# Seven block products in the first output projection, and partial results that accumulate in one bank

## The chip, the cores and the metric

The kernel runs on one core of a Trainium2 chip. The metric is device time in microseconds (us) of one execution. Engines in the profile are PE (TensorE matmul), PEld (TensorE weight load), DVE (VectorE), ACT (ScalarE), POOL (GpSimd) and SP (SyncE, which here only issues DMAs); `SPq` and `POOLq` are their DMA queues.

## The reference

Two layers on 528 tokens (16 learned ones ahead of 512) of width 2048. Each layer is `h + post_norm(mixer(pre_norm(h)))`, with RMS norms. Layer 0 is grouped-query attention with a gate, layer 1 a chunked gated linear attention. The part that the change touches is the last line of the attention, and the norm around it:

```
    return (o * jax.nn.silu(gate)) @ w_out                  # attention_mixer, w_out 2048 x 2048
    ...
        h = h + rmsnorm(y, post_norm[i])
```

`rmsnorm(y, w)` divides by the root of the mean square over the width, and multiplies by `w`.

## The kernel before

**Operands.** Activations lie transposed: width on the 128 partitions in 16 blocks (k), 528 tokens in the free dimension, in two halves of 264. Each is kept as two float32r parts: `uh`, the rounded value, and `ul`, the rest. A weight block is loaded in float32 (`wraw`, 512 KB, two buffers), and split by ScalarE into `whi` and by VectorE into `wlo` (three buffers each; `weights`, `split`). Every product is three matmuls: hi·hi, lo·hi and hi·lo.

**Plain columns.** `project` computes 128 output columns: for each token half 16 blocks of k by three matmuls into one of the three PSUM banks of `ps_p` (tag `pp`), and an evacuation.

**Seven products.** `seven` computes a pair of 128-column tiles for all tokens with a Strassen-Winograd scheme: the weight is cut into four 128x1024 blocks a11, a21, a12, a22 (columns by halves of k), the activation into four by halves of k and of the tokens. Sums and differences of the weight blocks are made by VectorE (`sums`), those of the activation once by `combine` (T1 to T4, split into `th`, `tl`). Seven block products, each 8 blocks of k by three matmuls of 128x264, replace eight. The results are added on VectorE (`add`) to SBUF tiles y1, y2. It is used for five pairs of the gate in layer 0 (about 106 to 208 us) and six pairs of values in layer 1 (about 1030 to 1152 us).

**Around the change.** The output projection of layer 0 runs from about 750 to 945 us. Its first two columns are a `group`: while it runs, the gated heads are reloaded from DRAM (`og_d`) and split into `uh`, `ul`, block by block. Columns 2 to 12 are plain. For columns 13 to 15 all first token halves come first and then all second halves, so that the norm of the first half can begin; the first three of their six weight units go to tiles of their own (`own`). For each column, `squares` copies the bank into `hs[m]` with the post-norm scale, squares it, and GpSimd adds the square to `acc`. Then `mean_rsqrt` and `residual` (which loads the old h through quarters of the tiles x0, x1) make the new h and its split, while layer 1's first columns are projected.

**Order.** The program is recorded by one pass; `clk` is a clock of estimated TensorE time that places the side work. A priority scheduler then fixes the order on each engine: weight loads and splits are recorded with a lead (`AHEAD`), so that they stand ahead of the work around them. An engine runs its instructions in that order and waits at each for its semaphores.

Of the kernel before, what the change touches and what calls it, by code (L numbers as in the profile page):

```python
# [19 lines left out]
P = 128  # L20
# [62 lines left out]
def hybrid_encoder(  # L83
# [22 lines left out]
    kq_d = scratch.tile([4, P, T], F32, name="kq_d")  # L106
    v_d = scratch.tile([5, P, D], F32, name="v_d")


# [9 lines left out]
    def col(i):  # L119
        return cols[:, i:i + 1]  # L120
# [71 lines left out]

    def combine(th, tl, xs):

        for k in range(KH):
            x = xs[k % len(xs)]
            u = [t[:, k:k + KH + 1:KH].bitcast(F32) for t in (uh, ul)]
            V.tensor_tensor(x.rearrange("p (j t) -> p j t", j=2), *u, op=ALU.add)
            q = x.rearrange("p (j t) -> p j t", j=4)
            V.tensor_tensor(q[:, 0:2], q[:, 1::2], q[:, 0:2], op=ALU.subtract)  # L200
            V.tensor_tensor(q[:, 3], q[:, 3], q[:, 0], op=ALU.subtract)
            V.tensor_tensor(q[:, 2], q[:, 2], q[:, 3], op=ALU.subtract)
            split(th[:, k], tl[:, k], x)
            yield 2.4

    def seven(src, c, ys, th, tl, free):

# [13 lines left out]
        def sums(o, a, b, op=ALU.subtract):  # L221
            with tc.high_priority(AHEAD):
                V.tensor_tensor(o, a, b, op=op)

        def product(w, b):
            ps = ps_p.tile([P, 512], F32, tag="pp", name="pp")[:, :HALF]
            bh, bl = b
            for k in range(KH):
                PE.matmul(ps, w[0][:, k], bh[:, k], start=k == 0, stop=False)  # L229
                PE.matmul(ps, w[0][:, k], bl[:, k], start=False, stop=False)  # L230
                PE.matmul(ps, w[1][:, k], bh[:, k], start=False, stop=k == KH - 1)  # L231
                clk.step(3 * (HALF + 7) / 2400)
            return ps
# [19 lines left out]
        A.copy(y1[:, l], product(w, of_u(0, 0)))  # L253
# [246 lines left out]
    fr = pool(la, "fr0")  # L500
    ps_s = pool(ps0, "ps_s", space=PSUM)
    ps_t = pool(ps0, "ps_t0", 2, space=PSUM)
    ps_o = pool(ps0, "ps_o", space=PSUM)

# [38 lines left out]
    for h in range(3, 13, 2):  # L543
        ys = y_tiles()
        free = seven(w_in0, 4096 + h * P, ys, th, tl, free)
        for i in range(2):
            nc.gpsimd.dma_start(out=g_d[h + i], in_=ys[i])
    clk.finish(first)
    clk.flush()
    la.close()  # L550


# [226 lines left out]
    yp = pool(la, "yp", 2)  # L779
    quarters = [yp.tile([P, 4 * HALF], F32, name=f"x{i}", bufs=1) for i in range(2)]  # L780


# [3 lines left out]
    hs = [tp.tile([P, T], F32, name=f"h{k}") for k in range(KT)]  # L786
    acc = tp.tile([P, T], F32, name="acc")
    r0 = tp.tile([P, T], F32, name="r0")
# [14 lines left out]
    def squares(m, ps, a, b):  # L803
        A.activation(hs[m][:, a:b], ps, AF.Copy, scale=col(POST + m))
        if m == 0:
            A.activation(acc[:, a:b], ps, AF.Square)
            return
# [6 lines left out]
    for m, ps, a, b in banks0:  # L814
        squares(m, ps, a, b)
    ps0.close()
    ps_g = pool(tr, "ps_g1", space=PSUM)
# [158 lines left out]
    sa = pool(la, "sa", 2)  # L976
    ps_v = pool(la, "ps_v", 2, space=PSUM)
    th, tl = [ta.tile([P, KH, 4 * HALF], F32R, name=f"t{w}") for w in "hl"]
    quarters += [ta.tile([P, 4 * HALF], F32, name=f"x{i}") for i in range(2, 4)]
# [34 lines left out]
    for vc in range(2, 14, 2):  # L1014
        ys = y_tiles()
        free = seven(w_in1, 2048 + vc * P, ys, th, tl, free)
        clk.drive(token_rows(ys, vc))
# [429 lines left out]
```

## Time and profile before

| | before |
|---|---|
| runs | 1787.76, 1788.43, 1789.2 us; median 1788.43 |
| span of the profiled execution | 1784.8 us, core clock 0.996 |
| TensorE / VectorE / ScalarE / GpSimd busy | 98% / 63% / 53% / 16% |
| bytes moved by DMA | 200.95 MB, 113 GB/s on average |

The profile was taken of one execution, whose span goes from the first to the last instruction; the runs' times contain some microseconds around it. In the groups of instructions, a line such as `L130 DVE TENSOR_TENSOR wlo<-wraw,whi 128x1024 ... x239 | 292.7, 1226 | 300.5 <-ACT whi L129 299.0` has the source line, the engine, the operation with output and inputs, the count, busy time in us, mean ns of one, and the idle time ahead of them with what ended it. In the DMA list the last number of a row is the median time in us from issue to landing.

### The profile page before, as it was taken

Reading aid. Unit: us, or ns where it says so; the run is one execution under the profiler, and the core shown is the slowest. Engines: PE = TensorE matmul, PEld = TensorE weight load, DVE = VectorE, ACT = ScalarE, POOL = GpSimd, SP = SyncE. Lnnn points to the kernel's source line nnn. Section 1 sums busy time; section 2 is a strip of 40 time slices with the busy share of each in tenths; the row PEclk is TensorE's granted clock in tenths of the full one; section 3 lists DMA queues with packets and bytes.
Section 4 is the critical chain, followed back from the end, with each engine's and each line's share of the span. In section 5 each row is a group of like instructions: output and inputs, shape, how many; then the busy total and the mean of one; then the engine's idle time right before and its main releaser. Section 6 shows DMA issues by size and latency. Waiting matters only on the chain.

```text
span 1784.8 us, 31606 instructions
## 1 busy us (share of the span) xinstructions
PE 1753.4 (98%) x12591; PEld 1653.0 (93%) x12591; DVE 1126.2 (63%) x1883; ACT 951.4 (53%) x1912; POOL 292.8 (16%) x392
## 2 busy tenths in 40 slices
PE   8999999999999999999999999999999999999998
PEld 8999999999999999999999899988888989888886
DVE  5888776667676666722247987667684865764224
ACT  5644455556556455632347444478685765853222
POOL 3113015323423322111111001110000000000000
PEclk9999999999999999999999999999999999999999
DMA  8444423223233233343336344343332332344333
GB/s 257 139 126 134 124 78 102 85 83 107 74 96 93 76 97 104 121 117 95 96 93 195 118 141 121 99 138 88 87 108 84 103 94 86 103 144 177 95 95 130
DMA packets 265124, 200.95 MB, mean 113 GB/s; under 512 B 9772, under 2 KB 239856, under 8 KB 264448
## 3 DMA queue, kind: packets, MB, share of 16 engines
q1 hardware_dynamic: 251600, 159.00, 31.1%
q0 software_dynamic: 13376, 39.93, 6.6%
q8 instruction: 99, 1.62, 0.4%
q14 instruction: 49, 0.40, 0.1%
HBM read 164.39 MB, written 28.01 MB: 108 GB/s over the span
## 4 chain that ended last, share of the span: by engine, by line
PE 75%; ACT 2%; DVE 2%; issue 1%; DMA 0%; POOL 0%; DVEq 0%; ACTq 0%; SPq 0%
PE pp L152 15%; PE pp L154 15%; PE pp L153 15%; PE f L1359 2%; PE f L1357 2%; PE f L1358 2%; PE pp L229 2%; PE pp L231 2%; PE pp L230 2%; PE pT L654 1%; PE o L1177 1%; PE o L1178 1%; PE o L1176 1%; PE s L636 1%; PE s L637 1%; PE s L638 1%
## 5 line engine op out<-in xcount | busy, mean ns | idle before, releaser
L152 PE MATMUL pp<-uh,whi 128*128 128x264 f32 (+1 forms) x2320 | 713.4, 308 | 1.0 <-POOL whi L363 0.9
L153 PE MATMUL pp<-ul,whi 128*128 128x264 f32 (+1 forms) x2320 | 703.1, 303 | 1.5 <-DVE ul L425 1.5
L154 PE MATMUL pp<-uh,wlo 128*128 128x264 f32 (+1 forms) x2320 | 703.6, 303 | 0.3 <-POOL wlo L364 0.3
L130 DVE TENSOR_TENSOR wlo<-wraw,whi 128x1024 fp32r<-128x1024 f32 (+1 forms) x239 | 292.7, 1226 | 300.5 <-ACT whi L129 299.0
L154 PEld LDWEIGHTS pp<-uh,wlo 128*128 128x128 f32 x2320 | 438.1, 189 | 17.5 <-POOL wlo L364 0.6
L152 PEld LDWEIGHTS pp<-uh,whi 128*128 128x128 f32 x2320 | 438.1, 189 | 17.4 <-POOL whi L363 1.2
L153 PEld LDWEIGHTS pp<-ul,whi 128*128 128x128 f32 x2320 | 438.6, 189 | 15.4 <-DVE ul L425 2.0
L129 ACT CAST whi<-wraw 128x1024 fp32r<-128x1024 f32 (+1 forms) x239 | 248.8, 1042 | 294.2 <-PE pp L153 108.7
L293 POOL DMA_DIRECT2D qs<-qw x96 | 48.3, 508 | 255.9 <-ACT sq L287 219.7
L129 ACT CAST whi<-x 128x1024 fp32r<-128x1024 f32 x48 | 50.2, 1049 | 58.7 <-PE pp L230 35.9
L644 ACT ACTIVATE pn<-s,mx 128x528 f32<-128x528 f32 (+1 forms) x72 | 50.2, 697 | 50.9 <-DVE mx L641 50.9
L231 PE MATMUL pp<-uh,wlo 128*128 128x264 f32 x264 | 75.2, 285 | 0.5 <-DVE wlo L130 0.5
L1359 PE MATMUL f<-whi,ul 128*128 128x512 f32 x192 | 75.6, 394 | 0.0
L1357 PE MATMUL f<-whi,uh 128*128 128x512 f32 x192 | 75.5, 393 | 0.0
L1358 PE MATMUL f<-wlo,uh 128*128 128x512 f32 x192 | 75.3, 392 | 0.0
L229 PE MATMUL pp<-uh,whi 128*128 128x264 f32 x264 | 75.0, 284 | 0.0
L230 PE MATMUL pp<-ul,whi 128*128 128x264 f32 x264 | 74.8, 283 | 0.0
L130 DVE TENSOR_TENSOR wlo<-x,whi 128x1024 fp32r<-128x1024 f32 x48 | 60.5, 1263 | 15.7 <-ACT whi L129 15.6
L641 DVE TENSOR_REDUCE mx<-s 128x1 f32<-128x528 f32 (+1 forms) x72 | 50.6, 703 | 28.7 <-PE s L638 28.1
L659 DVE TENSOR_TENSOR pl<-pT,ph 128x512 fp32r<-128x512 f32 (+1 forms) x80 | 47.3, 592 | 17.5 <-ACT ph L658 16.7
L229 PE MATMUL pp<-th,whi 128*128 128x264 f32 x192 | 56.1, 292 | 0.8 <-ACT th L129 0.8
L658 ACT CAST ph<-pT 128x512 fp32r<-128x512 f32 (+1 forms) x80 | 40.8, 510 | 29.0 <-PE pT L654 24.6
(413 smaller groups left out, 3762.7 us busy)
## 6 DMA issues: line engine op xcount, KB each, us to landing
wraw<-in_attn_w_in_dram SPq DMA_DIRECT2D x82, 512.0 KB, 4.1
wraw<-in_gla_w_in_dram SPq DMA_DIRECT2D x81, 512.0 KB, 3.9
wraw<-in_attn_w_out_dram SPq DMA_DIRECT2D x32, 512.0 KB, 3.8
wraw<-in_gla_w_out_dram SPq DMA_DIRECT2D x32, 512.0 KB, 3.8
x<-in_gla_w_in_dram SPq DMA_DIRECT2D x15, 512.0 KB, 4.1
qs<-qw POOLq DMA_DIRECT2D x96, 66.0 KB, 3.9
x<-in_attn_w_in_dram SPq DMA_DIRECT2D x12, 512.0 KB, 4.6
x<-h_d SPq DMA_DIRECT2D x32, 132.0 KB, 3.5
```

Of the source, the lines that this page charges most:

```text
L129: A.copy(hi, src)
L130: V.tensor_tensor(lo, src, hi.bitcast(F32), op=ALU.subtract)
L152: PE.matmul(ps, wh, uh[:, k, a:b], start=first, stop=False)
L153: PE.matmul(ps, wh, ul[:, k, a:b], start=False, stop=False)
L154: PE.matmul(ps, wl, uh[:, k, a:b], start=False, stop=last)
L229: PE.matmul(ps, w[0][:, k], bh[:, k], start=k == 0, stop=False)
L230: PE.matmul(ps, w[0][:, k], bl[:, k], start=False, stop=False)
L231: PE.matmul(ps, w[1][:, k], bh[:, k], start=False, stop=k == KH - 1)
L641: V.reduce_max(mx, s, axis=AX.XY, negate=True)
L1357: PE.matmul(ps, uh[:, k, ts], wh[:, kk], start=(k == 0), stop=False)
L1358: PE.matmul(ps, uh[:, k, ts], wl[:, kk], start=False, stop=False)
L1359: PE.matmul(ps, ul[:, k, ts], wh[:, kk], start=False, stop=(k == KT - 1))
```

## The change

Three things are done.

1. Layer 0's output columns 5 to 12 become four pairs by `seven`. `combine` gets its operands in part from DRAM: for the first six of the eight k, GpSimd's queue loads the two raw blocks from `og_d` into x0, x1 and two more tiles, while columns 0 to 4 are still computed plainly.
2. The raw outputs of columns 0 to 12 are copied to tiles y0, y1, squared from there, and stored to a scratch tensor `y_d`. After the pairs they are loaded into `hs`, whose memory is used by the pairs' operands until then. The post-norm scale moves to `residual`. The first loads of the old h, the loads for the low-rank gates (`wr`) and the memset of `wl` come behind the pairs.
3. In `seven`, for all 15 pairs, products that share partial sums accumulate in a bank: P1, T2, T3 and T4 in one bank of `pp` (p1), with a copy or an addition out of it after each, and T1 and the last difference in a bank of new pools (`ps_x`, tag `x`, p5).

```diff
-    def combine(th, tl, xs):
-
+    def combine(th, tl, xs, raw=None, n_raw=0, pace=2.4):
+
+        def load(k):
+            if k < n_raw:
+                nc.gpsimd.dma_start(out=xs[k % len(xs)].rearrange("p (j t) -> p j t", j=2),
+                                    in_=raw[k:k + KH + 1:KH].rearrange("j p t -> p j t"))
+        for k in range(len(xs)):
+            load(k)
         for k in range(KH):
...
-            V.tensor_tensor(x.rearrange("p (j t) -> p j t", j=2), *u, op=ALU.add)
+            if k >= n_raw:
+                V.tensor_tensor(x.rearrange("p (j t) -> p j t", j=2), *u, op=ALU.add)
...
-            yield 2.4
-
-    def seven(src, c, ys, th, tl, free):
+            load(k + len(xs))
+            yield pace
+
+    def seven(src, c, ys, th, tl, free, ps_x):
...
-        w = parts(a11)
+        w1 = parts(a11)
         sums(s, a21, a22, ALU.add)
+        w5 = parts(s)
         sums(a21, a11, a21)
         sums(a11, s, a11)
-        A.copy(y1[:, l], product(w, of_u(0, 0)))
-        add(y1[:, r], product(parts(a11), of_t(T2)), y1[:, l])
-        add(y2[:, r], product(parts(a21), of_t(T3)), y1[:, r])
-        add(y2[:, l], product(parts(a22), of_t(T4)), y2[:, r])
-        p5 = product(parts(s), of_t(T1))
-        add(y2[:, r], p5, y2[:, r])
+        w2 = parts(a11)
+        p1 = ps_p.tile([P, 512], F32, tag="pp", name="pp")[:, :HALF]
+        product(w1, of_u(0, 0), p1)
+        A.copy(y1[:, l], p1)
+        p5 = product(w5, of_t(T1))
+        A.copy(y2[:, r], p5)
+        product(w2, of_t(T2), p1, True)
+        A.copy(y1[:, r], p1)
+        add(y1[:, l], product(parts(a12), of_u(1, 0)), y1[:, l])
+        sums(a11, a12, a11)
+        product(parts(a21), of_t(T3), p1, True)
+        add(y2[:, r], p1, y2[:, r])
+        product(parts(a11), of_u(1, 1), p5, True)
         add(y1[:, r], p5, y1[:, r])
-        w = parts(a12)
-        sums(a11, a12, a11)
-        add(y1[:, l], product(w, of_u(1, 0)), y1[:, l])
-        add(y1[:, r], product(parts(a11), of_u(1, 1)), y1[:, r])
-        return [spare, a21, a22, s, a12, a11]
+        product(parts(a22), of_t(T4), p1, True)
+        A.copy(y2[:, l], p1)
+        return [spare, s, a21, a11, a12, a22]
...
+    ys = [y_tile(i) for i in range(2)]
+    for m, ps, a, b in banks0:
+        A.copy(ys[m][:, a:b], ps)
+        outgoing(m, ys[m], a, b)
+    ps0.close()
+    ps_x = pool(sx, "ps_x2", 4, space=PSUM)
+    built = clk.drive(combine(th, tl, xs, og_d, 6, 3.0))
+    for m in range(2, 5):
+        y = y_tile(m % 2)
+
+        def plain(ps, a, b):
+            A.copy(y[:, a:b], ps)
+            outgoing(m, y, a, b)
+        project(w_out0, m * P, HALVES, plain)
+    clk.finish(built)
+    free = [wpool.tile([P, 1024], F32, tag="wraw", name="wraw", bufs=2) for _ in range(2)]
+    free += [q[:, :1024] for q in xs]
+    for m in range(5, KT - 3, 2):
+        ys = [y_tile(i) for i in range(2)]
+        free = seven(w_out0, m * P, ys, th, tl, free, ps_x)
+        for i in range(2):
+            outgoing(m + i, ys[i], 0, T)
+    sx.close()
...
+    for m in range(KT - 3):
+        nc.gpsimd.dma_start(out=hs[m], in_=y_d[m])
...
-        A.activation(hs[m][:, a:b], ps, AF.Copy, scale=col(POST + m))
...
+        A.copy(hs[m][:, a:b], ps)
...
-        V.tensor_tensor(h, h, r0[:, a:b], op=ALU.mult)
+        V.scalar_tensor_tensor(h, h, col(POST + k), r0[:, a:b], op0=ALU.mult, op1=ALU.mult)
...
-    for m in range(2, KT - TAIL):
-        project(w_out0, m * P, HALVES, evac)
```

`outgoing` squares a part of y, adds the square to `acc` on GpSimd, and stores y to `y_d` when it is complete.

The order of ScalarE where the last plain or paired column gives way to column 13. Before (own0h to own2h are the three first weight units of columns 13 to 15, split into their own tiles; the L804 and L809 rows evacuate columns 10 to 12):

```order
L129 CAST own0h<-wraw 128x1024
L804 ACTIVATE h_9630<-pp,cols 128x264
L809 ACTIVATE sq<-pp 128x264
L129 CAST whi<-wraw 128x1024
L129 CAST own1h<-wraw 128x1024
L804 ACTIVATE h_9630<-pp,cols 128x264
L809 ACTIVATE sq<-pp 128x264
L129 CAST own2h<-wraw 128x1024
L129 CAST whi<-wraw 128x1024
L804 ACTIVATE h_9631<-pp,cols 128x264
```

and now (y_10705 and y_10706 are the outputs of the last pair, L280 the copy of its last product):

```order
L272 COPY y_10705<-pp 128x264
L130 CAST whi<-wraw 128x1024
L816 ACTIVATE sq<-y_10705 128x528
L280 COPY y_10706<-pp 128x264
L816 ACTIVATE sq<-y_10706 128x528
L130 CAST own0h<-wraw 128x1024
L130 CAST own1h<-wraw 128x1024
L130 CAST own2h<-wraw 128x1024
L130 CAST whi<-wraw 128x1024
L868 COPY h_10950<-pp 128x264
```

The casts of the own units, which stood among the evacuations of columns 11 and 12, now follow the copy of the last product and the square of the last output.

The order of ScalarE between the group of columns 0 and 1 and column 2, now (uh rows are the splits of the reloaded heads, sh rows the casts of the activation sums, L823 the copies of column 0's banks):

```order
L130 CAST uh<-o_sb 128x528
L130 CAST sh<-x_9591 128x1056
L130 CAST whi<-wraw 128x1024
L130 CAST sh<-x_9592 128x1056
L130 CAST whi<-wraw 128x1024
L130 CAST sh<-xs_9599 128x1056
L130 CAST sh<-xs_9600 128x1056
L823 COPY y_9601<-pp 128x264 x2
```

Before, the evacuation of column 0 followed the splits and the next weight unit's cast directly; four casts of sums now stand between.

The order of VectorE inside the pair of columns 7 and 8, now (y0_10257 and y1_10258 are its outputs, pp_10278 the bank that accumulates, px_10359 and px_10304 banks of the other pool; xs1_9600 is first a difference of blocks and then, from L232, the next pair's sum):

```order
L131 TENSOR_TENSOR wlo_10416<-xs1_9600,whi_10415 128x1024
L232 TENSOR_TENSOR xs1_9600<-wraw_10031,x1_9592 128x1024
L247 TENSOR_TENSOR y0_10257<-px_10359,y0_10257 128x264
L131 TENSOR_TENSOR wlo_10445<-wraw_10032,whi_10444 128x1024
L232 TENSOR_TENSOR wraw_10031<-x0_9591,wraw_10031 128x1024
L247 TENSOR_TENSOR y1_10258<-pp_10278,y1_10258 128x264
L131 TENSOR_TENSOR wlo_10488<-x0_9591,whi_10487 128x1024
L232 TENSOR_TENSOR x0_9591<-xs1_9600,x0_9591 128x1024
L247 TENSOR_TENSOR y0_10257<-px_10304,y0_10257 128x264
```

The addition out of the accumulating bank stands behind two sums of the next pair's weight blocks and a split.

More of the change, by code (lines that the diff above doesn't have):

```diff
@@ L107, in hybrid_encoder @@
     v_d = scratch.tile([5, P, D], F32, name="v_d")
+    y_d = scratch.tile([13, P, T], F32, name="y_d")
     with tc.high_priority():
@@ L223, in sums, with product @@
                 V.tensor_tensor(o, a, b, op=op)
[L225 to L226 removed]
+        def product(w, b, ps=None, more=False):
+            if ps is None:
+                ps = ps_x.tile([P, 512], F32, tag="x", name="px")[:, :HALF]
             bh, bl = b
             for k in range(KH):
[L229 to L231 removed]
+                PE.matmul(ps, w[0][:, k], bh[:, k], start=k == 0 and not more, stop=False, skip_group_check=more)
+                PE.matmul(ps, w[0][:, k], bl[:, k], start=False, stop=False, skip_group_check=more)
+                PE.matmul(ps, w[1][:, k], bh[:, k], start=False, stop=k == KH - 1,
+                          skip_group_check=more)
                 clk.step(3 * (HALF + 7) / 2400)
@@ L780, in hybrid_encoder, with y_tile, outgoing @@
     quarters = [yp.tile([P, 4 * HALF], F32, name=f"x{i}", bufs=1) for i in range(2)]
+    acc = yp.tile([P, T], F32, name="acc", bufs=1)
+    sx = ExitStack()
+    xp = pool(sx, "xp")
+    th, tl = [xp.tile([P, KH, 4 * HALF], F32R, name=f"s{w}") for w in "hl"]
+    xs = quarters + [xp.tile([P, 4 * HALF], F32, name=f"xs{i}") for i in range(2)]
+    def y_tile(i):
+        return yp.tile([P, T], F32, tag=f"y{i}", name=f"y{i}")
+    def outgoing(m, y, a, b):
+        if m == 0:
+            A.activation(acc[:, a:b], y[:, a:b], AF.Square)
+        else:
+            sq = xp.tile([P, T], F32, tag="sq", name="sq", bufs=2)[:, :b - a]
+            A.activation(sq, y[:, a:b], AF.Square)
+            G.tensor_tensor(acc[:, a:b], acc[:, a:b], sq, op=ALU.add)
+        if b == T:
+            nc.gpsimd.dma_start(out=y_d[m], in_=y)
+    ys = [y_tile(i) for i in range(2)]
[20 more added lines that the diff above has]
+    sx.close()
     tr = ExitStack()
```

17 lines of the change are left out of this document (6 added, 11 removed).

## The prediction

> **What bounds the kernel now.** I read the page's shares first, then busy time by stretch around the places that the change touches, then TensorE's waits there. The page's first two parts:
>
> ```profile
> PE 1753.4 (98%) x12591; PEld 1653.0 (93%) x12591; DVE 1126.2 (63%) x1883; ACT 951.4 (53%) x1912; POOL 292.8 (16%) x392
> ...
> PEclk9999999999999999999999999999999999999999
> ```
>
> TensorE is busy for 98% of the span at an unthrottled clock. Busy time by stretch (columns: span, then busy us and instructions of PE, PEld, DVE, ACT, POOL, clock, DMA share, GB/s):
>
> ```profile
> 800.00:850.00 50.00, 50.00 (x414) 50.00 (x413) 9.80 (x8) 14.84 (x26) 8.31 (x9) 1.00 0.32 92
> 850.00:900.00 50.00, 50.00 (x413) 50.00 (x413) 13.59 (x11) 16.92 (x27) 7.82 (x8) 1.00 0.37 106
> 105.00:208.00 103.00, 101.60 (x830) 100.76 (x829) 83.92 (x99) 45.61 (x57) 27.91 (x33) 1.00 0.39 115
> ```
>
> The output projection (first two rows) is pure TensorE work: 50.00 us / 414 = 0.1208 us per matmul, and the waits of PE between 740 and 900 us have no row at all. So a matmul removed there is worth its 0.1208 us, and a wait added there is paid in full. In the gate pairs, which already use seven products (third row), VectorE is busy for 83.92 of 103 us. The waits of PE in the two stretches of pairs, 105 to 208 and 1030 to 1160 us:
>
> ```profile
> PE ssq L518 <- DVE shl L130: 0.7, 1, 0.7
> PE pp L231 <- DVE wlo L130: 0.5, 1, 0.5
> PE pp L229 <- ACT th L129: 0.8, 1, 0.8
> ```
>
> The eleven present pairs lose 2 us in all; reordering them can gain no more than that.
>
> **Term 1, fewer products: −11.6 us.** A pair of columns costs 2 x 2 x 16 x 3 = 192 matmuls plainly and 7 x 8 x 3 = 168 with seven products. Four pairs save 96, and 96 x 0.1208 = 11.6 us.
>
> **Term 2, from the last pair to column 13: about +10.2 us.** Before, the three first weight units of columns 13 to 15 were split while column 12 was projected. Now their buffers begin where the pairs' operands end, and ScalarE's cast of own0h stands behind the copy of the last product and the 128x528 square of it. Durations, one row from the page's groups and the others from the groups between 100 and 210 us:
>
> ```profile
> L130 DVE TENSOR_TENSOR wlo<-wraw,whi 128x1024 fp32r<-128x1024 f32 (+1 forms) x239 | 292.7, 1226 | 300.5 <-ACT whi L129 299.0
> ...
> L129 ACT CAST whi<-wraw 128x1024 fp32r<-128x1024 f32 x15 | 15.6, 1049 | 24.5 <-DVE wraw L223 9.8 <-PE pp L230 9.8 <-PE pp L153 4.4
> L236 DVE TENSOR_TENSOR y<-pp,y 128x264 f32<-128x264 f32 x34 | 14.0, 425 | 4.1 <-ACT y L253 2.1 <-PE pp L231 2.0
> L223 DVE TENSOR_TENSOR x<-wraw,x 128x1024 f32<-128x1024 f32 x4 | 4.9, 1226 | 6.7 <-DMA x<-in_attn_w_in_dram 6.7
> L547 POOL DMA_DIRECT2D g_d<-y x9 | 5.1, 563 | 35.8 <-DVE y L236 35.6 <-issue 0.2
> L133 ACT ACTIVATE sq<-sq 128x528 f32<-128x528 f32 x3 | 1.9, 649 | 4.2 <-DVE sq L519 4.2
> L253 ACT COPY y<-pp 128x264 f32<-128x264 f32 x5 | 1.9, 379 | 10.7 <-DMA g_d<-y 8.4 <-DVE sq L519 2.3
> ```
>
> Count from t, the moment at which the last product leaves TensorE. A ScalarE evacuation follows the last matmul's slot by about 0.25 us, as these two rows show (770.84 + 0.12 to 771.21):
>
> ```profile
> 770.84 0.29 PE L154 MATMUL pp<-uh,wlo 128*128 128x264 f32 x1
> ...
> 771.21 0.48 ACT L804 ACTIVATE h<-pp,cols 128x264 f32<-128x264 f32 x1 [3.82 <-PE pp L154]
> ```
>
> Copy to t+0.6, square to t+1.2, own0h to t+2.25, own0l (1.2) to t+3.5. The third matmul of a k needs own0l, two matmuls fit ahead of it, so column 13 loses about 3.35 us. Own0l also frees one of the only two raw buffers: the load for column 14's first unit is issued at t+3.55, and with a landing time D, a cast and a split it is ready at t+3.55+D+2.2. Column 13's first half (48 matmuls, 5.8 us) ends at t+9.15: the second stall is D−3.4 (two matmuls again start early). Column 15's first unit follows in the same buffer, D' after column 14's split, against another 5.8 us: D'−3.35.
>
> What is D? Undisturbed, the page's first row below. But POOL issues the reloads of the 13 raw outputs in that very stretch: its last addition to acc ends near t+2.7 (square 1.2, addition about 1.4 as L624 below), the store of y12 is issued by t+3.3, and then 13 loads of 264 KB at 0.56 us each, from t+3.3 to t+10.6. The nearest thing in the trace is the start of the last stage, where POOL loads of 1 MB run beside a weight load:
>
> ```profile
> wraw<-in_attn_w_out_dram SPq DMA_DIRECT2D x32, 512.0 KB, 3.8
> ...
> wraw<-in_gla_w_out_dram SPq DMA_DIRECT2D x1, 512.0 KB, 9.4
> ...
> q0 software_dynamic: 236, 1.80, 76.3%
> q1 hardware_dynamic: 237, 0.49, 22.6%
> ...
> wraw<-in_gla_w_out_dram SPq DMA_DIRECT2D x1, 512.0 KB, 8.6
> ```
>
> (the page's list, window 1612 to 1618, then 1618 to 1624). The two queues moved 236 and 237 packets there: turn about, packet for packet, and the weight load took 9.4 and 8.6 us. Bounds for D: 3.8, and 12.2 from the rival below. I take 9.4, the row it is nearest to, because the reloads overlap its whole flight: second stall 6.0. For D' I take 4.2, the reloads being nearly over: 0.85. Sum 3.35 + 6.0 + 0.85 = 10.2 us; with D = 3.8 for both it is 4.2.
>
> **Term 3, the group before column 2: +0.3 us.** In ScalarE's order four casts of the raw sums (sh) now precede the copy of column 0's bank, which column 2 needs. Their loads are issued behind the memset of ups and land late (POOL's timeline before, with an addition of 128x528 above and the wr load and wl memset below it, and a row of the page's DMA list):
>
> ```profile
> 752.17 1.33 POOL L624 TENSOR_TENSOR gs<-gs,gr 128x528 f32<-128x528 f32 x1 [15.30 <-DVE ul L130]
> 755.99 0.52 POOL L777 MEMSET ups<- 80x512 f32 x1 [2.48 <-DVE ul L130]
> ...
> 757.42 1.22 POOL L792 DMA_DIRECT2D wr<-in_gla_w_in_dram  x1
> 758.64 1.83 POOL L794 MEMSET wl<- 128x2048 f32 x1
> ...
> h<-h_d POOLq DMA_DIRECT2D x4, 1024.0 KB, 10.2
> ```
>
> Four loads of 528 KB, issued at 0.56 us each from 756.5 to 758.8 us, should end near 766.5 (2.1 MB at the 381 GB/s of window 1618 to 1624, 5.7 us, and some 2 us of start); three subtractions and a cast for each, 770.0 on VectorE, 771.75 on ScalarE, so the copy starts near 772.1 where TensorE is ready at 772.0. At the 13 us of a 1 MB load the price would be 5.
>
> **Term 4, one bank for partial results, 15 pairs: +0.7 us in all.** The bank must be read out within the one product (24 x 0.1208 = 2.9 us) that lies between two uses. The tightest reader is VectorE's addition after T3, which stands behind the next pair's sum, and that waits for its a22. Its buffer is that of product 5's weights, whose split starts when product 2 ends, 5.8 us into the pair: issue at 5.8 + 0.25 + 1.05 + 1.2 = 8.3, then landing D, sum 1.2, addition 0.4, split 1.2, sum 1.2, addition 0.4: done at 12.7 + D, against product 7's start at 6 x 2.9 = 17.4. So it costs nothing up to D = 4.7. The landings of the pairs:
>
> ```profile
> x<-in_gla_w_in_dram SPq DMA_DIRECT2D x15, 512.0 KB, 4.1
> ...
> x<-in_attn_w_in_dram SPq DMA_DIRECT2D x12, 512.0 KB, 4.6
> ...
> 177.02 8.96 SPq L210 DMA_DIRECT2D x<-in_attn_w_in_dram  x2
> ...
> 182.87 1.23 DVE L223 TENSOR_TENSOR x<-wraw,x 128x1024 f32<-128x1024 f32 x1 [2.65 <-DMA x<-in_attn_w_in_dram]
> ```
>
> Medians below 4.7, but one of the loads that SP issued from 177.02 on was still waited for until 182.87, some 5.6 us after its issue, which would cost 0.9. One such pair, less a little: 0.7. Bounds: −0.5 (the wlo wait goes) and 0.9 x 15 = 13.5.
>
> **Term 5, +0.5 us**: layer 1's first pair waits 0.8 for th before; that cast now also stands behind a cast whose load is later, 1.3. **Nothing** for the rest: the scale in the residual runs as scalar_tensor_tensor on the same 128x264 tile, the y_d stores are POOL work with POOL 16% busy, and the reloads, wr and the wl memset are wanted only when the first halves of columns 13 to 15 are projected, 3 x 5.8 = 17.4 us and the stalls after t. Without that cover wr's issue and the memset would cost 1.22 + 1.83 = 3 us.
>
> Sum: −11.6 + 10.2 + 0.3 + 0.7 + 0.5 = +0.1 us on a span of 1784.8. The runs' median lies 3.6 above this span, so I forecast **1788.5 us**.
>
> [...]
>
> **Rivals.** (a) *The reloads hardly disturb the refill*, D from 3.8 to 5: Term 2 is 4.2 to 6.6, and the time 1782.5 to 1785. For it: the stores and loads are spread by POOL's 0.56 us issues. Against it: 264 KB per 0.56 us is 480 GB/s, above the 381 measured. (b) *Packet for packet*, with the small packets of this weight matrix (windows 800 to 850 and 960 to 970 us; packets, MB, share of 16 engines):
>
> ```profile
> q1 hardware_dynamic: 8984, 4.53, 31.6%
> ...
> q0 software_dynamic: 319, 1.05, 26.4%
> ```
>
> One of 512 bytes takes 0.316 x 50 x 16 / 8984 = 0.028 us, one of POOL's 0.264 x 10 x 16 / 319 = 0.132. A weight load has 64 on each engine; if each waits for one of POOL's, 64 x 0.16 + 2.0 = 12.2 us, Term 2 is 13.0 and the time 1791.3. (c) *Slower: bank p1 holds TensorE in most pairs.* It decides from D above 4.7 in the next pair's a22; at 5.2 it is 0.5 us in each of 15, 7.5 for my 0.7, and 1795.3. For it: VectorE's 83.92 of 103 us in the gate pairs and the 6.7 us that four sums waited for loads. Against it: the medians. (d) *Column 0's copy waits 5 us for late raw sums*: 1793.2. (e) That the change doesn't remove the products is excluded by TensorE's order.
>
> **How the numbers follow.** Forecast 0.37, (a) 0.28, (b) 0.14, (c) 0.14, (d) 0.07. Two runs' medians closer than 0.2% (3.6 us) can't be told apart here, so faster is below 1784.9 and slower above 1792.0. Faster: nearly all of (a) and the low edge of the forecast, 0.31. Slower: (c), most of (d), the edge of (b) and of the forecast, 0.25. Same: 0.44. The forecast alone spans 1785 to 1792 (D 5 to 11); with both signs held the range reaches from (a)'s 1782 to (c)'s 1795.5.
>
> **What would show it.** Right: waits of PE on own0l and on the splits of columns 14 and 15 of some 3, 6 and 1 us, weight landings of 8 us or more beside the h loads, 96 fewer matmuls at 0.12 us, and no PE wait in the pairs' first product after a copy. Wrong: landings near 4 there (then a), PE waits on L247 or L280 spread over the pairs (c), or a PE wait on the copy of y0 near 772 us (d). The forecast fails altogether if stalls elsewhere in the attention or gate stages appear.

## The result and the profile after

| | before | after |
|---|---|---|
| runs | 1788.10 us median (1785.29 to 1789.2, 4 runs) | 1802.09 us median (1800.18 to 1806.67, 4 runs) |
| span of the profiled execution | 1784.8 us | 1799.8 us (a run of 1801.52) |

The change makes the kernel slower: the ratio is 1.0077, with a 95% interval of 1.0058 to 1.0097. The forecast was 1788.5 us with a range up to 1795.5, so the time lies outside it. The page's first two parts for the changed kernel:

```profile
PE 1749.2 (97%) x12495; PEld 1647.1 (92%) x12495; DVE 1177.0 (65%) x1913; ACT 978.2 (54%) x1957; POOL 319.5 (18%) x416
...
PEclk9999999999999999999989999999999999999999
```

The 96 matmuls are gone (12591 to 12495). But TensorE's idle time, span less busy time, grew from 31.4 to 50.6 us: +19.2. And its busy time fell by 4.2 us only, where 96 x 0.1208 = 11.6 were removed. Most of the difference of 7.4 us is a slower clock (worked out below): the strip of clocks has an 8 where the strip before had only nines. So 19.2 − 11.6 + 7.4 = +15.0 us, the whole growth of the span. Three things must be found: the new gaps, the stretches at half clock, and what ties them together.

**The stretch after the last pair.** Busy time by stretch (span; busy us and instructions of PE, PEld, DVE, ACT, POOL; clock; DMA share; GB/s), after, one row in the pairs and one behind them:

```profile
800.00:850.00 50.00, 50.00 (x414) 50.00 (x414) 32.47 (x29) 21.97 (x31) 8.04 (x9) 1.00 0.40 117
893.00:931.00 38.00, 27.58 (x177) 26.22 (x177) 9.59 (x12) 10.05 (x17) 15.65 (x21) 0.82 0.65 197
```

and before, in the same place of the program:

```profile
895.00:930.00 35.00, 35.00 (x287) 34.87 (x286) 9.99 (x20) 10.34 (x22) 4.56 (x5) 1.00 0.30 86
```

The four pairs themselves run without a gap (no PE wait has a row between 800 and 893 us). Behind them TensorE now idles for 10.4 of 38 us at a mean clock of 0.82. PE's waits there, after (us in all, times, longest):

```profile
PE pp L153 <- ACT whi L130: 5.2, 1, 5.2
PE pp L153 <- ACT own0h L130: 2.1, 1, 2.1
PE pp L155 <- DVE own0l L131: 1.1, 1, 1.1
PE pp L155 <- DVE own2l L131: 0.8, 1, 0.8
PE pp L153 <- ACT own2h L130: 0.7, 1, 0.7
PE pp L155 <- DVE wlo L131: 0.5, 1, 0.5
```

Own0 is the first unit of column 13, own2 the first of column 14, and whi/wlo hold the second of column 14. ScalarE's casts of the three (start, duration, the wait ahead in brackets), and GpSimd's reloads:

```profile
896.57 1.03 ACT L130 CAST own0h<-wraw 128x1024 fp32r<-128x1024 f32 x1
...
906.17 1.05 ACT L130 CAST own2h<-wraw 128x1024 fp32r<-128x1024 f32 x1 [7.62 <-DMA wraw<-in_attn_w_out_dram]
...
917.14 1.04 ACT L130 CAST whi<-wraw 128x1024 fp32r<-128x1024 f32 x1 [9.92 <-DMA wraw<-in_attn_w_out_dram]
```

```profile
898.07 5.47 POOL L851 DMA_DIRECT2D h<-y_d  x10
```

The trace's DMA events give each weight load in this stretch:

```
issued 899.25  landed 906.15   6.90 us   column 14, first unit
issued 900.38  landed 917.12  16.73 us   column 14, second unit
issued 908.50  landed 918.43   9.93 us
issued 919.47  landed 923.37   3.90 us
```

The second load was issued 1.1 us behind the first and landed 11 us behind it. What the two queues moved in 906 to 909 us, behind the first landing (packets, MB, share of 16 engines; the software queue carries GpSimd's transfers, on the pages 50.21 MB for 39.93 before, the hardware queue the weights, 159.00 MB in both):

```profile
q0 software_dynamic: 288, 0.98, 88.3%
q1 hardware_dynamic: 288, 0.15, 17.1%
```

That is as many packets of 512 bytes as of 3.4 KB: the weights got 50 GB/s. In 901 to 906 us it was 313 against 1123 packets, so the first load still came through faster; in 909 to 917 us it was 418 against 1667, so the turns were not even for the rest of the second load's flight either. From the last product to the second half of column 13 TensorE has 17.4 us of work at full clock and took 34.23: 16.8 us lost. Of these 10.4 are gaps, about 4.8 are half clock (worked out below), and the last 1.6 fit the edges of the six gaps.

**The half clock.** It comes in whole windows of 3.4 us (but for the program's last moments, the trace's clock stands at 0.50 for 3.413 us or 6.827 at a time). Three rows of busy time by stretch, after; the window from 905.78 to 909.20 us, also at clock 1.00, is left out between the second and the third:

```profile
899.00:902.36 3.36, 3.09 (x14) 3.09 (x15) 1.35 (x2) 0.00 (x0) 3.36 (x8) 0.50 0.85 208
902.36:905.78 3.42, 3.42 (x30) 3.42 (x30) 0.00 (x0) 0.00 (x0) 1.04 (x2) 1.00 1.04 361
...
909.20:912.60 3.40, 3.40 (x18) 3.40 (x17) 0.00 (x0) 0.00 (x0) 2.98 (x2) 0.50 1.07 344
```

A full-clock window with 30 matmuls stands between windows with 14 and 18 at 0.50. Where the rate changes, the times fit one grid of 3.41 us, and what precedes a window at half clock here is one in which TensorE idled for much of it: 2.90 us ahead of 898.95, 3.02 ahead of 916.02, 2.06 ahead of 721.46. The half-clock window from 916.02 itself held 2.60 us of idle time, and a second one followed, to 922.84. In the profiles of before and after, windows with 1.64 to 1.81 us idle were not followed by half clock, but one of 1.49 (ahead of 909.19) was. The kernel before had this too, in two windows of its attention stage:

```profile
352.30:355.70 3.40, 1.40 (x12) 1.16 (x10) 1.95 (x4) 2.40 (x5) 0.00 (x0) 1.00 0.57 154
355.70:362.50 6.80, 5.64 (x26) 5.57 (x27) 4.80 (x12) 5.24 (x14) 1.89 (x2) 0.50 0.37 117
```

In all, apart from the last moments of the program, the clock is at one half for 20.5 us after and 6.8 before, and TensorE is busy for 17.2 and 5.7 us of them. A matmul starts every 0.22 us there (at 909.27, 909.49 and 909.71, for example), where it is every 0.1208 at full clock, so 45% of that busy time is lost: 5.2 us more than before, out of the 7.4. The other 2.2 fit the edges of gaps, of which there are ten more (40 above 0.05 us for 30): by the trace, the matmul ahead of a gap lasts its full 0.28 us instead of a slot of 0.12, and the first one behind it mostly holds its slot for 0.23 (907.27 to 907.49, for example).

**The pairs that were there before.** PE's waits of more than 0.4 us in 105 to 212 us (gates of layer 0), 740 to 800 (columns 0 to 4) and 1030 to 1165 us (values of layer 1), after:

```profile
PE pp L239 <- DVE y L247: 2.9, 2, 2.3
...
PE pp L155 <- DVE wlo L131: 1.2, 1, 1.2
...
PE px L239 <- ACT th L130: 2.1, 1, 2.1
```

The first is what rival (c) described: a product that accumulates in bank p1 waits until VectorE's addition has read it. Before, none of the three stretches had a wait above 0.8. Behind the output projection there are three more gaps, which no term had: 1.1 us at 951.8, 0.7 at 977.4 and 1.5 at 1183.3 us, where the kernel before had none above 0.6 us between 900 and 1240 except the 0.8 of the first value pair. No run was made for these.

### The profile page after: what moved, and what is told of

Same layout as the page of the kernel before. It is cut to its first block, busy times and chain, and to the rows that moved or that the text cites. A ratio compares the mean times of both kernels' runs of the same rounds, so it can differ in the third digit from the quotient of the medians.

```text
span 1799.8 us, 31575 instructions
## 1 busy us (share of the span) xinstructions
PE 1749.2 (97%) x12495; PEld 1647.1 (92%) x12495; DVE 1177.0 (65%) x1913; ACT 978.2 (54%) x1957; POOL 319.5 (18%) x416
## 3 DMA queue, kind: packets, MB, share of 16 engines
q1 hardware_dynamic: 251600, 159.00, 31.0%
q0 software_dynamic: 16320, 50.21, 8.2%
## 5 line engine op out<-in xcount | busy, mean ns | idle before, releaser
L153 PE MATMUL pp<-uh,whi 128*128 128x264 f32 (+1 forms) x2064 | 641.8, 311 | 5.8 <-ACT whi L130 5.2
L155 PE MATMUL pp<-uh,wlo 128*128 128x264 f32 (+1 forms) x2064 | 632.0, 306 | 2.0 <-DVE wlo L131 1.6
L154 PE MATMUL pp<-ul,whi 128*128 128x264 f32 (+1 forms) x2064 | 631.3, 306 | 2.2 <-DVE ul L442 2.2
L153 PEld LDWEIGHTS pp<-uh,whi 128*128 128x128 f32 x2064 | 390.7, 189 | 22.5 <-ACT whi L130 5.5
L155 PEld LDWEIGHTS pp<-uh,wlo 128*128 128x128 f32 x2064 | 390.6, 189 | 19.6 <-DVE wlo L131 2.4
L154 PEld LDWEIGHTS pp<-ul,whi 128*128 128x128 f32 x2064 | 391.4, 190 | 16.0 <-DVE ul L442 2.6
L131 DVE TENSOR_TENSOR wlo<-x,whi 128x1024 fp32r<-128x1024 f32 x57 | 73.5, 1290 | 35.3 <-ACT whi L130 35.3
L659 DVE TENSOR_REDUCE mx<-s 128x1 f32<-128x528 f32 (+1 forms) x72 | 50.6, 703 | 28.0 <-PE s L656 27.4
L239 PE MATMUL px<-uh,whi 128*128 128x264 f32 x240 | 68.4, 285 | 0.0
L241 PE MATMUL px<-uh,wlo 128*128 128x264 f32 x240 | 68.3, 284 | 0.0
L240 PE MATMUL px<-ul,whi 128*128 128x264 f32 x240 | 67.9, 283 | 0.0
```

The source lines that it names most:

```text
L131: V.tensor_tensor(lo, src, hi.bitcast(F32), op=ALU.subtract)
L153: PE.matmul(ps, wh, uh[:, k, a:b], start=first, stop=False)
L154: PE.matmul(ps, wh, ul[:, k, a:b], start=False, stop=False)
L155: PE.matmul(ps, wl, uh[:, k, a:b], start=False, stop=last)
L239: PE.matmul(ps, w[0][:, k], bh[:, k], start=k == 0 and not more, stop=False, skip_group_check=more)
L240: PE.matmul(ps, w[0][:, k], bl[:, k], start=False, stop=False, skip_group_check=more)
```

## The experiments

Each ran beside the kernel before on the same chip, and the difference in the table is against that kernel's median there: 1788.10 for the change itself, 1789.0 for the four runs below it, 1788.64 for the next four, 1788.63 for earlier reload and one bank in the output pairs, 1788.57 for one bank in the value pairs.

| kernel | median (lowest to highest), us | against before, us | ratio, 95% interval |
|---|---|---|---|
| the change | 1802.09 (1800.18 to 1806.67) | +14.0 | 1.0058 to 1.0097 |
| pairs only | 1796.0 (1792.86 to 1799.41) | +7.0 | 1.0025 to 1.0054 |
| old pairs | 1795.53 (1794.2 to 1797.73) | +6.5 | 1.0023 to 1.0049 |
| late reload | 1793.56 (1790.15 to 1797.12) | +4.6 | 1.0017 to 1.0037 |
| fill | 1800.35 (1800.16 to 1807.98) | +11.4 | 1.0050 to 1.0091 |
| both | 1789.3 (1783.2 to 1792.03) | +0.7 | 0.9991 to 1.0010 |
| swapped buffers | 1785.16 (1782.53 to 1787.97) | −3.5 | 0.9972 to 0.9991 |
| no rotation products | 1799.57 (1795.0 to 1801.19) | +10.9 | 1.0038 to 1.0072 |
| raw loads held | 1786.83 (1784.76 to 1789.49) | −1.8 | 0.9979 to 0.9998 |
| earlier reload | 1783.8 (1779.76 to 1785.21) | −4.8 | 0.9958 to 0.9981 |
| one bank in the output pairs | 1782.49 (1780.15 to 1783.38) | −6.1 | 0.9950 to 0.9975 |
| one bank in the value pairs | 1791.28 (1788.29 to 1793.2) | +2.7 | 1.0001 to 1.0021 |

**The change in two halves.** Pairs only puts the change's order of products and its bank, with the pools that they need, into the eleven pairs of the kernel before. Old pairs is the changed kernel with the old `seven` in all 15 pairs. The edit of the one is that of the other reversed:

```diff
-        A.copy(y1[:, l], product(w, of_u(0, 0)))
-        add(y1[:, r], product(parts(a11), of_t(T2)), y1[:, l])
...
+        product(w1, of_u(0, 0), p1)
+        A.copy(y1[:, l], p1)
+        p5 = product(w5, of_t(T1))
+        A.copy(y2[:, r], p5)
+        product(w2, of_t(T2), p1, True)
+        A.copy(y1[:, r], p1)
...
```

> The kernel before with the new order and the accumulating bank in its eleven present pairs, and the old output projection. Theory 'the bank costs': the trace of the change has 2.0 us more TensorE gaps among the gate pairs and 1.3 more ahead of the value pairs than before, so this kernel is 3 us slower than before, about 1791.5, with waits on L247 in the gate pairs. Rival 'the gaps there come from the run, not from the order': within 1 us of before, 1787 to 1789.

> The change with the old order of products and three rotating banks in all 15 pairs; four output pairs, the store and the reload stay. Theory 'the bank costs 3 us': about 1798.5. Rival 'everything is lost between the last pair and column 15': within 1 us of the change, 1801 to 1803.

Measured: +7.0 us for the new order and its bank in eleven pairs, and 14.0 − 6.5 = 7.5 us come back when all 15 pairs go without them. Both expectations had only 3 us. The order and the bank were not tried apart. The waits of PE in 105 to 212 and in 1030 to 1165 us of pairs only (its profile is of a run of 1799.41 us) are much like those of the change, with one more on the bank in a value pair:

```profile
PE pp L230 <- DVE y L238: 2.5, 1, 2.5
...
PE px L230 <- ACT th L129: 2.2, 1, 2.2
PE pp L230 <- DVE y L238: 1.0, 1, 1.0
```

TensorE's waits in the pairs grew by 4.0 us, and windows at half clock stand right behind the two largest, from 148.3 and from 1046.0 us, which cost another 3.0 by the working above. The expectations had counted the waits without the clock. So half of the loss is Terms 4 and 5, which the forecast had at 1.2 us together. The stretch behind the last pair hardly depends on it: 31.92 us in old pairs.

**The stretch behind the pairs.** Late reload leaves the stretch's transfers to the weights: a copy of one column of acc into each target holds its load until GpSimd has added column 14's first half to acc. The load of wr, and the casts that follow it, are held in the same way.

```diff
-    for m in range(KT - 3):
-        nc.gpsimd.dma_start(out=hs[m], in_=y_d[m])
-    nc.gpsimd.dma_start(out=wr, in_=w_in1[:, :, 6144:6176])
...
+    def late_loads():
+        G.tensor_copy(wr[:, 0, :1], acc[:, :1])
+        nc.gpsimd.dma_start(out=wr, in_=w_in1[:, :, 6144:6176])
...
+        for m in range(KT - 3):
+            G.tensor_copy(hs[m][:, :1], acc[:, :1])
+            nc.gpsimd.dma_start(out=hs[m], in_=y_d[m])
...
+            if m == KT - 2 and part[0] == 0:
+                late_loads()
```

> The change with the 13 reloads of raw outputs and the wr load held back until GpSimd has added column 14's first half. Theory 'reloads contend with the weight units': the two units of column 14 land in about 4 us each instead of 6.9 and 16.7, the gaps between the last pair and column 15 fall from 10.4 to about 4 us, one of the four half-clock windows there stays, and the time is about 1792. Rival 'the two raw buffers and the late own splits set the pace': landings shorten but the gaps stay near 9 us, 1800 or more.

Fill keeps the reloads where they are, and gives TensorE 26, 12 and 44 matmuls whose result nobody reads, where it waits for the three units. This is to keep the clock up without changing a transfer.

```diff
+                if fill and k in fill[1]:
+                    for _ in range(fill[1][k]):
+                        PE.matmul(fill[0], uh[:, 0, :P], uh[:, 0, a:b], start=True, stop=True)
...
+            fills = {13: {0: 26}, 14: {0: 12, 8: 44}}.get(m) if part[0] == 0 else None
```

> The change with 82 extra matmuls into an unused bank where TensorE idled: 26 ahead of column 13, 12 ahead of column 14, 44 ahead of its second weight unit (they add no result). Theory 'the half clock costs in full': the four half-clock windows there vanish and the time falls by the 5.3 us they took, to 1797. Rival 'the half clock is mostly hidden, because the second unit's landing ends the stall anyway': only the windows behind that landing count, about 2 us, 1800. If the clock does not follow idle time: 1802 and the windows stay.

The stretch by the same view, late reload and then fill:

```profile
893.00:931.00 38.00, 34.06 (x259) 33.11 (x258) 13.93 (x23) 13.22 (x24) 18.43 (x36) 0.96 0.62 197
```

```profile
893.00:931.00 38.00, 35.02 (x281) 33.96 (x280) 9.93 (x12) 10.05 (x17) 15.66 (x21) 1.00 0.69 208
```

With the reloads away, the weight loads landed in 4.80, 5.14, 3.83 and 4.90 us, the wait on whi is gone, and 22.91 us replace 34.23. The program gained 14.0 − 4.6 = 9.4 us: contention with the loads that were held is shown. Fill brought the clock to 1.00, but the stretch only from 34.23 to 31.64 us, because the second unit of column 14 is as late as before; the half clock ahead of that landing was mostly hidden by it. Its time does not tell a gain of 2.6 us from none (the intervals overlap).

**Both.** Late reload and old pairs together:

> The change with the old order of products in all 15 pairs and with the reloads and wr held back. If the two losses are separate, they add up: the old order alone saved 6.5 us and the late reload 8.5, so 15 of the 14 lost come back and it stands at 1787, within 2 us of before. Rival 'both shorten the same stall': no better than the better of the two, 1793.

+0.7 us, no difference that can be told. The two savings, 7.5 and 9.4, give 13.3 together, 3.6 less than their sum. What is left in the stretch (24.14 us for 17.4 of work) is the stall on own0, 2.7 + 0.7 us, and two windows at half clock right behind its first part, from 898.4 us, which cost some 2.8. Nothing has been gained by the 11.6 us of products yet.

**The stall on own0.** It exists because the three first units of columns 13 to 15 have tiles of their own, whose memory the pairs' operands hold until the last product. Swapped buffers is both, with the first three units in the common buffers, where they can be split during the last pair, and the last three in the tiles of their own:

```diff
-                kept[m] = [weights(w_out0[:, k0:k0 + 8, m * P:(m + 1) * P], own=own.pop(0) if own else None)
+                kept[m] = [weights(w_out0[:, k0:k0 + 8, m * P:(m + 1) * P], own=own.pop(0) if (m, k0) > (KT - 2, 0) else None)
```

> As e5_both, and the first three weight units of columns 13 to 15 go to the three common buffers, which are free as soon as products 5, 6 and 7 of the last pair end, and the last three to the tiles of their own. Theory 'own0h waits for the end of the pairs': the stall of about 3.4 us ahead of column 13 and the half-clock window behind it (1.7 us) go, 1782, which is faster than before. Rival 'the raw buffers hold column 13 back too': no change against e5_both.

The stretch took 17.50 us, its 17.4 of work, and the kernel is now faster than before by 3.5 us, not by the 6 to 7 that were expected. A new wait has come (waits of PE, 893 to 945 us), with a window at half clock behind it, from 932.0 us; that the reloads are now late for their own readers is the reading that earlier reload tries below:

```profile
PE ht L920 <- issue: 3.0, 2, 2.4
```

**What holds the bank in the gate pairs.** VectorE's instructions in the pair that lost 2.3 us, after (start, duration), and GpSimd's beside them:

```profile
142.35 1.23 DVE L232 TENSOR_TENSOR x<-wraw,x 128x1024 f32<-128x1024 f32 x1 [2.44 <-DMA x<-in_attn_w_in_dram]
143.49 0.43 DVE L247 TENSOR_TENSOR y<-px,y 128x264 f32<-128x264 f32 x1
143.84 2.01 DVE L232 TENSOR_TENSOR wraw<-x,wraw 128x1024 f32<-128x1024 f32 x1
145.78 2.33 DVE L131 TENSOR_TENSOR wlo<-wraw,whi 128x1024 fp32r<-128x1024 f32 x1
148.02 0.42 DVE L247 TENSOR_TENSOR y<-pp,y 128x264 f32<-128x264 f32 x1
```

```profile
143.08 1.69 POOL L311 TENSOR_TENSOR qw<-qw,cos 128x528 f32<-128x528 f32 x1 [1.84 <-DMA qs<-qw]
144.73 2.29 POOL L312 TENSOR_TENSOR qs<-qs,sin 128x528 f32<-128x528 f32 x1
147.10 2.17 POOL L313 TENSOR_TENSOR qw<-qw,qs 128x528 f32<-128x528 f32 x1
```

The addition that frees p1 (the last row of VectorE's) stands behind a sum of 2.01 and a split of 2.33 us. GpSimd works on the first heads' rotation at just that time; from 128 to 140 us, between two groups of its products, each sum and split took 1.22 or 1.23. No rotation products is the changed kernel without the three products of the rotation for the first three heads; their transfers stay, and so one key head and two query heads are left unrotated:

```diff
-    def rotate(qw, qs):
+    def rotate(qw, qs, products=True):
...
+        if not products:
+            return
```

> The change without GpSimd's three products of the rotation for the first three heads (the rotation is left out there, its DMAs stay). Theory 'VectorE's splits and sums take 2.0 to 2.4 us instead of 1.2 beside a GpSimd product, and that makes the addition out of bank p1 late in the second gate pair': no instruction of 2 us or more there, the gap of 2.3 us near 148.6 us is gone and the time is 2 to 4 us below the change, about 1799. Rival 'a late landing of the next pair's a22 does it': the gap stays above 1.5 us, 1802.

No wait of PE is left in 105 to 212 us, and VectorE's same instructions read:

```profile
139.10 1.23 DVE L232 TENSOR_TENSOR x<-wraw,x 128x1024 f32<-128x1024 f32 x1 [0.65 <-DMA x<-in_attn_w_in_dram]
...
140.59 1.22 DVE L232 TENSOR_TENSOR wraw<-x,wraw 128x1024 f32<-128x1024 f32 x1
141.72 1.22 DVE L131 TENSOR_TENSOR wlo<-wraw,whi 128x1024 fp32r<-128x1024 f32 x1
```

GpSimd's products make the 2.01 and 2.33 us, and without them the wait is gone. The sum's wait for its load is shorter here too (0.65 for 2.44 us; the load landed in 3.74 us where it took 4.90), so how much of the 2.3 us comes from each is not told apart by this run. The kernel gained 14.0 − 10.9 = 3.1 us, with intervals that overlap.

**The group before column 2.** Raw loads held is swapped buffers with the third and fourth load of raw sums held back behind column 0's square, so that the casts of late sums do not stand ahead of column 0's copy:

```diff
+                if k in (2, 3):
+                    G.tensor_copy(xs[k][:, :1], after[:, :1])
```

> As e6_swap_own, and the third and fourth load of raw sums wait for the square of column 0's output, so that their casts cannot stand ahead of the copy of its bank. Theory 'late raw sums hold that copy': no gap ahead of column 2 and none in column 3, 1 to 3 us below e6_swap_own, about 1780. Rival 'that gap moves into column 5, since the sums end later': equal to e6_swap_own.

It is not faster (−1.8 against −3.5 us, overlapping). The waits of PE in 770 to 810 us, swapped buffers and then raw loads held:

```profile
PE pp L155 <- DVE wlo L131: 1.2, 1, 1.2
PE pp L153 <- ACT y L814: 0.9, 1, 0.9
```

```profile
PE pp L155 <- DVE wlo L131: 3.5, 2, 2.0
PE pp L153 <- ACT y L816: 0.4, 1, 0.4
```

The wait on ScalarE's copy falls from 0.9 to 0.4 us, but the waits on VectorE's splits, at columns 3 and 4, come to 3.5 us for 1.2: the sums are the same work, only later. Term 3's place was right, its price of 0.3 too small, and this is no cure.

**A faster version.** Earlier reload is swapped buffers with the reloads let go one column sooner, at column 13's addition to acc, the load of wr not held at all, and the casts of wl recorded behind column 14. One bank in the output pairs adds the change's order and bank in the four output pairs alone:

```diff
-            if m == KT - 2 and part[0] == 0:
-                late_loads()
+            if part[0] == 0 and m < KT - 1:
+                (late_loads if m == KT - 3 else late_wl)()
...
-        free = seven(w_out0, m * P, ys, th, tl, free)
+        free = seven_acc(w_out0, m * P, ys, th, tl, free, ps_x)
```

> As e6_swap_own, but the reloads start after the addition of column 13's first half, 5.8 us earlier, and wr is loaded right behind the pairs again. e6_swap_own has a new TensorE gap of 2.4 us and one of 0.5 on the transposes (ht) near 931 us, behind the residual that waits for the reloads, and a half-clock window behind it. Theory 'the reload is now too late': these go, 2.9 + 1.7 = up to 4.6 us, 1781 to 1782. Rival 'an earlier reload meets the weight loads of columns 14 and 15 again': gaps of 2 us or more ahead of them, 1785 or more.

> As e9_earlier, and the four output pairs alone use the new order with the accumulating bank; gate and value pairs keep the old. GpSimd has no product to compute during most of them (only additions of 128x528 to acc), and weight landings are 3.8 to 4.1 us. Theory 'the bank costs only where VectorE is slowed or a landing passes 4.7 us': within 1.5 us of e9_earlier. Rival 'the order itself costs': 0.4 us or more in each of four pairs, 1.6 us or more slower, with gaps on L247 or on the copies in all four.

Measured: −4.8 and −6.1 us. The second is the best of all, 0.9962 of the time before. Between the two no difference can be told (their ranges overlap), so no cost of the bank is seen in the output pairs, and it is not shown to help. Earlier reload itself is not told apart from swapped buffers (−3.5 us, overlapping intervals). Its wait at the transposes (ht) fell from 3.0 to 1.2 us and the window at half clock there went, but it has gaps of 1.3 and 0.8 us ahead of column 15's second unit. The rival expected such gaps from late weights, but the weights had landed in 3.9 us: ScalarE's cast of them stood behind the casts of wl, and those waited for the load of wr, 6.4 us under way. PE's waits in 893 to 931 us, one bank in the output pairs:

```profile
PE pp L155 <- DVE own2l L131: 0.8, 1, 0.8
PE pp L153 <- ACT own2h L130: 0.2, 1, 0.2
```

**The value pairs.** The kernel before with the new order and its bank in layer 1's six value pairs alone splits the +7.0 of pairs only:

> The kernel before with the new order in the six value pairs alone (gates and output projection as before). e1_pairs_only, with it in all eleven pairs, was 7 us slower. Theory 'the gate pairs pay most, since GpSimd computes beside them': the value pairs cost what their trace showed, 1.4 us more ahead of the first pair and 1 us near 1125, 2.4 us and at most one half-clock window of 1.7, so 1791 to 1793. Rival 'the order costs alike everywhere': six elevenths of 7, 1793, with gaps in most pairs.

+2.7 us. Its one large wait in 1030 to 1165 us stands at the first value pair:

```profile
PE px L290 <- ACT th L129: 2.5, 1, 2.5
```

This wait is for the cast of th, not for the bank. A window at half clock follows, 1041.3 to 1044.8 us. So the six value pairs cost 2.7 us, nearly all in one place, and about 4.3 of the 7.0 are left to the five gate pairs; both differences are uncertain by some 2 us, so this is a rough share.

## Why the prediction was wrong, point by point

**What bounds the kernel, and Term 1, right.** In 800 to 850 us TensorE is busy for all of the time with 414 matmuls, 0.1208 us each, and 96 fewer make 11.6 us. The best version, 6.1 us faster than before, shows that this gain can be had in part.

**Term 2, right in its mechanism, wrong in which load is late and, for want of the clock, in its size: the largest miss, 6.6 us.** The first stall is 2.1 + 1.1 = 3.2 us for 3.35. The second was to be 6.0, with D = 9.4; the first unit of column 14 landed in 6.9 us and cost 1.5. The gaps sum to 10.4 for 10.2, but this is a coincidence: 5.7 of them are the wait for column 14's second unit, 16.7 us under way, which the working did not price. It followed the first load down to its split and let the load issued behind it on the same queue pass as covered. What rival (b) supposed, a packet of one queue for a packet of the other, fits the counts for part of its flight: 288 and 288 packets in 906 to 909 us. But 313 to 1123 in 901 to 906 is not turn about, and no run here shows why. With some 4.8 us of half clock and 1.6 at the gaps' edges on top, the stretch lost 16.8 us, 6.6 more than forecast.

**Term 4, the step that failed most for its size: 0.7 us forecast, about 4.3 measured** (7.0 in pairs only, less the 2.7 of the value pairs, which is Term 5's wait). Rival (c), at 0.14, had the right wait, on L247, but not its place: it put 0.5 us into each of 15 pairs. That its 7.5 us is also what old pairs saved is luck. The formula 12.7 + D against 17.4 took every sum and split at 1.2 us. In the gate pairs they take 2.0 to 2.3 beside GpSimd's products, and the load of a22 in the pair shown above landed in 4.90 us: 12.7 + 4.9 + 0.8 + 1.1 = 19.5 against 17.4 makes a wait of 2.1, and 2.3 was measured. So the formula held in this pair, and its durations were wrong. The profile before showed this, in rows that were not read for it: groups in 100 to 210 us, and one split beside a rotation product.

```profile
L130 DVE TENSOR_TENSOR wlo<-x,whi 128x1024 fp32r<-128x1024 f32 x21 | 27.6, 1314 | 4.4 <-ACT whi L129 4.4
...
L223 DVE TENSOR_TENSOR x<-x,x 128x1024 f32<-128x1024 f32 x4 | 6.9, 1734 | 0.1
...
121.94 2.29 DVE L130 TENSOR_TENSOR wlo<-x,whi 128x1024 fp32r<-128x1024 f32 x1 [0.18 <-ACT whi L129]
```

A mean of 1734 ns where 1226 is the plain duration says that some of the four took far longer. The prediction took the split's 1226 from the row of the whole program, and the sum's from the one group of this stretch that had the plain duration. (The sum and the split took 2.01 and 2.33 us beside GpSimd's products and 1.22 each in the run without them; by what means the products slow them is not shown.) The price is not spread over 15 pairs either: it sits in few pairs, with none seen in the output pairs.

**Term 5, right place, too small.** Forecast +0.5 for the first value pair; its wait grew from 0.8 to 2.1 us, and one of 2.5 with the window at half clock behind it goes with the 2.7 us of the run that has the new order in the value pairs alone.

**Term 3, right place, too small.** Forecast 0.3; 1.6 us in two gaps (0.4 on the copy, 1.2 on a split). The 2 us of start in its working, and in rival (b)'s, were the author's estimate; in the DMA list of before, the small loads of vt took 1.9 us for 16 KB and 2.0 for 32 KB from issue to landing.

**No term at all for the clock.** The prediction read "unthrottled" from the strip, whose slices are 45 us long and hide a window of 3.4. The profile before had such windows after 355.7 us. About 5 of the 15 us by which the span grew came in this way, and they are not additive: fill removed the half clock from one stretch and gained at most 2.6. Rivals (a) and (d) did not occur. The changes of the attention stage (+0.6 us of gaps) and of the start (+1.0), and the three gaps behind the output projection, are not shown to be the change's. In sum, the misses of Term 2 (6.6 us), Term 4 (3.6), Term 5 (2.2) and Term 3 (1.3) make 13.7 us, and the median lies 13.6 above the forecast. The match is closer than the runs allow.

## What to carry to other kernels

A stretch in which the bounding engine has no slack is priced by every load that is queued in it, not by the first one that is late: here 5.7 of the 10.4 us of gaps were the wait for the load issued second. Transfers which are not yet wanted should be held until those that are wanted have landed: with the 13 reloads of 264 KB and the load of wr held, the four weight loads landed in 3.83 to 5.14 us, where the two of column 14 had taken 6.90 and 16.73, and 9.4 us came back. Before a bank or a buffer is given a deadline of one product, take the durations of its readers from the stage they will run in, with what the neighbouring engine does at that moment (2.01 and 2.33 us here), and not from the page's mean (1.23). Putting the freed work in is one half of such a change; here the gain came only when the transfers and the buffers around it were set anew as well: +14.0 us against before became −4.8 and −6.1.

## What the runs showed of the hardware that was not expected

- TensorE's clock stood at one half for whole windows of 3.41 us, in the change behind windows in which TensorE had idled for only 1.49 to 3.02 us, and once behind one without work. Over all 13 profiles, from about 10 us on and without the program's last 25 us, all 41 full-clock windows with 1.93 us idle or more were followed by one at half clock, 7 of the 32 with 1.45 to 1.92, and none with less. Of the windows that were themselves at half clock, all six with 0.63 us idle or more were followed by another, and none with 0.60 or less.
- The same gap was followed by half clock in some profiles and not in others. The gap of some 2.06 us near 720 us, in code that no kernel here alters, is followed by half clock in the profiles of after, pairs only, late reload, both and no rotation products, and not in those of before, old pairs, fill, swapped buffers, raw loads held, earlier reload, one bank in the output pairs and one bank in the value pairs. In after it lies whole in one window (718.04 to 721.46 us, 2.06 idle), in before in two (1.81 us in the first, 0.25 in the second). Such gaps would fit the spread of 3 us either way that many of these kernels have among their runs, and a run's mean clock goes with its time (of the ten runs of both, 0.996 in the one of 1783.2 us and 0.993 in the one of 1792.03); that they make this spread, and that the place in the window decides, is not shown.
- Of two 512 KB weight loads issued 1.1 us apart on one queue, beside loads of 264 KB on GpSimd's, the first took 6.9 us and the second 16.7, where the median of the 32 loads of this weight before is 3.8. What let the first through so much better (313 to 1123 packets in its last 5 us, then 288 to 288) is open.
